# Modulation products of layer 0 issued for four weight pieces at a time

## The chip, the cores and the metric

The kernel runs on one core of one Trainium2 chip. The metric is the device time of one execution in microseconds (us); less is better. Three runs of the kernel before gave 1642.43 us in the median, 1640.19 at the lowest and 1645.79 at the highest.

## The reference, cut to what matters

Two layers work on 256 latent tokens (x) and 256 context tokens (ctx), each of 1024 channels. Every layer begins with the modulation: six vectors of 1024 for the latents and six for the context, which are products of one activated row each with the weight w_ada (1024 x 6144 for a layer).

```python
c_act = jax.nn.silu(c)
cc_act = jax.nn.silu(c_ctx)
for l in range(DEPTH):
    m_l = jnp.split((c_act @ w_ada[l] + b_ada[l])[:, None, :], 6, axis=-1)
    m_c = jnp.split((cc_act @ w_ada[l] + b_ada[l])[None, None, :], 6, axis=-1)
    h_l = modulate(rms_norm(x, norm_g[l, 0]), m_l[0], m_l[1])
    h_c = modulate(rms_norm(ctx, norm_g[l, 0]), m_c[0], m_c[1])
    y_l, y_c = token_mixer(h_l, h_c, w_in[l], ...)
    x = x + m_l[2] * rms_norm(y_l, norm_g[l, 1])
    h_l = modulate(rms_norm(x, norm_g[l, 2]), m_l[3], m_l[4])
    x = x + m_l[5] * rms_norm(sq_relu_mlp(h_l, w_mlp_up[l], w_mlp_down[l]), norm_g[l, 3])
```

The first two of the six vectors are needed before the token mixer, the other four only behind it. The token mixer runs three branches over one input projection: a gated linear recurrence (HGRN, 4 heads), differential attention (4 heads, two softmaxes each) and sliding-window attention; their gated outputs are merged and projected.

## The kernel before, in words

**Dense products.** A weight block of 2048 columns is loaded as two halves by SP's queue (L218). ACT copies the high part (`L227`), DVE takes the rest (`L228`), and TensorE runs three products for each tile of 128 channels (L249 to L251 with channels as output rows, L261 to L263 with tokens). These dense products fill PE nearly all the time. They write two banks of the accumulator in turn (`b_84`, `b_85` in the order listings); a bank can be written again when ACT has copied its content out.

**Mixers.** Beside the dense products of the next block run the chains of a mixer, issued by generators that take turns. The HGRN head walks seven levels: ACT copies (L776), PE multiplies (L783 on five levels, 32x32 groups; L786 on two, 128x128), DVE rescales in place what PE just read (L800), then the next level may start; L828 and L841 follow. The two heads of a pair run abreast. A differential head takes for each token tile two pairs of score products (L937, L938), a maximum (DVE L977), an exponential (ACT L898), the scaling and difference on DVE (L980, L981, L983), transposes (PE L989) and their copy (ACT L991). These small products use the other banks, `b_86` to `b_90`.

**Modulation.** Columns of w_ada come in three groups of 2048. Group 0 of layer 0 is done at the start. Groups 1 and 2 are spread over the weight blocks of layer 0's mixers: `weights` ends with `pump` (L349), which runs one entry of a list. An entry is one piece of w_ada, 128 rows by 1024 columns: `ada_load` (L385) takes two units of 512 columns from the arena A (33 units) and issues the load on SP's queue, and `ada_step` (L360) issues four products of 32x256 (L365), one for each column group j, into four row groups of the bank `b_91`. Every product is two instructions in the trace, so a piece is eight. After 16 pieces, `ada_done` (L428) copies the bank out. There are 34 entries (16 pieces and a done, twice) and 34 blocks.

**Order.** The arena gives out the units that were freed longest ago, in the order of the program; a unit that was freed by an instruction late in the program makes its next writer wait for it. The order in which each engine issues is made when the program is built: a scheduler takes the program's instructions as their inputs and buffers come ready. High priority (`hp`) moves evacuations and weight splits ahead.

Of the kernel before, what the change touches and what calls it, by code (L numbers as in the profile page):

```python
# [17 lines left out]
PSUM = bass.MemoryType.PSUM  # L18

D = 1024  # L20
T = 512
LAT = 256
DEPTH = 2
EPS = 1e-6
UNIT = 512
RAWS = 5
AHEAD = 100

O_DQ, O_DK, O_DV = 0, 512, 1024
# [83 lines left out]
class Net:  # L113
    def __init__(self, ctx, tc, ins, out):
        self.tc, self.nc = tc, tc.nc
        self.I, self.out = ins, out
        nc = self.nc
# [35 lines left out]
        self.exps = []  # L153
        self.pumps = []
        self.rate = 1
        self.ps = [pp.tile([128, 512], F32, tag=f"b{i}", name=f"b{i}") for i in range(8)]
# [23 lines left out]

# [1 line left out]
    def raw_slot(self):  # L182
# [4 lines left out]
    def set_fence(self, ops, skip, count):  # L187
        """the splits of weight blocks skip .. skip + count - 1 from here on are traced behind ops"""
        self.fence = [skip, count, ops]
# [7 lines left out]
    def weights(self, pieces, rope=0, dst=None):  # L197
        """a block of 2048 columns, loaded in halves; pieces(half): (view fn of the half, source AP); the first `rope`
        columns, in groups of 64 (axis, half, 16), are taken as (half, axis, 16)"""
        nc, tc = self.nc, self.tc  # L200
        if dst is None:
            self.wi += 1
            c = (self.wi % 2) * 4096
# [38 lines left out]
    def mm_cm(self, ps, w, nk, cc, act, t0, n, kt0=0, start=True, stop=True):  # L242
        """ps[128 channels, n tokens] = w[:, cc:cc+128]^T act"""
        nc = self.nc
        hi, lo = w
        for k in range(nk):
            xh, xl = act[kt0 + k]
            wh, wl = hi[:, k, cc:cc + 128], lo[:, k, cc:cc + 128]
            nc.tensor.matmul(ps, wh, xh[:, t0:t0 + n], start=start and k == 0, stop=False)  # L249
            nc.tensor.matmul(ps, wh, xl[:, t0:t0 + n], start=False, stop=False)  # L250
            nc.tensor.matmul(ps, wl, xh[:, t0:t0 + n], start=False, stop=stop and k == nk - 1)  # L251

    def mm_tm(self, ps, w, nk, c0, n, act, tt, kt0=0, start=True, stop=True):
        """ps[128 tokens, n] = act[:, tt]^T w[:, c0:c0+n]"""
        nc = self.nc
        hi, lo = w
        for k in range(nk):
            xh, xl = act[kt0 + k]
            xh, xl = xh[:, tt * 128:tt * 128 + 128], xl[:, tt * 128:tt * 128 + 128]
            wh, wl = hi[:, k, c0:c0 + n], lo[:, k, c0:c0 + n]  # L260
            nc.tensor.matmul(ps, xh, wh, start=start and k == 0, stop=False)  # L261
            nc.tensor.matmul(ps, xh, wl, start=False, stop=False)  # L262
            nc.tensor.matmul(ps, xl, wh, start=False, stop=stop and k == nk - 1)  # L263

# [1 line left out]
    def setup(self):  # L266
# [92 lines left out]

    def ada_step(self, l, g, half, k):  # L360
        nc = self.nc
        ca = self.CA.rearrange("p (k m) -> p k m", m=32)
        raw = self.ada_load(l, g, half, k)
        for j in range(4):
            nc.tensor.matmul(self.ps[7][32 * j:32 * j + 32, half * 256:half * 256 + 256], ca[:, k, :],  # L365
                             raw[:, j * 256:(j + 1) * 256], start=k == 0, stop=k == 7)
        raw.free()

    def ada_late(self, l, groups, ahead=2):
        """the groups of layer l on the vector engine; each step loads for a later one"""  # L370
        todo = [(g, half, k) for g in groups for half in range(2) for k in range(8)]
# [21 lines left out]
    def ada_acc(self, raw, k, acc):  # L393
        """sums over k of w * silu(c), by partition, one for each stream"""
        ca = self.CA.rearrange("p (k m) -> p k m", m=32)
# [49 lines left out]
    def mvec(self, l, s, i):  # L445
        """stream s: 0 latents, 1 context"""
        return self.M[l][:, s * 48 + i * 8:s * 48 + i * 8 + 8]

# [1 line left out]
    def rstd(self, ms, cols, add=True):  # L450
        """ms: mean squares, to which EPS is added unless it is in them"""
        r = self.sm(cols)
# [5 lines left out]
    def scale_vecs(self, l, sub, q=None):  # L458
        """of all channel tiles, or of q and 4 + q"""
        nc = self.nc  # L460
# [10 lines left out]
    def first_norm(self):  # L471
        """normalized and transposed x, channel tile k -> [128, 512]"""
        nc = self.nc
# [39 lines left out]
    def first_blocks(self, offs, evacs):  # L513
        """the first blocks of w_in[0]; channel tiles q and 4 + q are multiplied as soon as their modulation is known"""
        nc, tc = self.nc, self.tc
# [44 lines left out]
    def prenorm(self, tt, yb):  # L560
        """x[tt] / rms, transposed: the PSUM tiles of channels 0..511 and 512..1023"""
        nc = self.nc
# [23 lines left out]
    def modulate(self, tt, sv, tiles, yb, ops=(), quick=False):  # L586
        """the tiles of prenorm() to the activation of tokens tt; traced behind ops"""
        nc = self.nc
# [35 lines left out]
    def post(self, tt, y, yss):  # L624
        """x += y / rms, where y already holds the gains; yss [128, 5]: the shares of y's quarters in the mean
        square, and EPS"""
        nc = self.nc
# [9 lines left out]
    def tm_out(self, w, r0, act, y, yss, seqs, add, gains=None, after=None):  # L637
        """y[tt] (+)= act^T w[r0:r0 + 1024]; seqs: lists of (tokens, column blocks) worked through in turn; with gains,
        the mean squares of y are taken and y becomes y * gains(tt)"""
        nc = self.nc  # L640
# [25 lines left out]

# [1 line left out]
    def hgrn_dense(self, l, w, hp):  # L668
        """heads 2 hp and 2 hp + 1"""
        nc, A = self.nc, self.A  # L670
# [58 lines left out]
    def tm_pair(self, w, off, dst=None):  # L729
        """buffers, token tiles [128, 256] in them, and the function that fills those of a range"""  # L730
        bufs, v = self.pair_bufs(range(4))
# [13 lines left out]
    def hgrn_head(self, l, hd, s, v, gn, ys):  # L745
        """generator: one step of the chain at a time"""
        nc, A = self.nc, self.A
# [115 lines left out]
    def readout(self, ps, tiles, gain, ys):  # L863
        """per-tile rms norm of ps[128 tokens, tile, 128], gain, transpose, split"""
        nc, A = self.nc, self.A
# [29 lines left out]

# [1 line left out]
    def exp(self, out, in_, **kw):  # L897
        self.exps = self.exps[-3:] + [self.nc.scalar.activation(out, in_, AF.Exp, **kw)]  # L898

    def rope(self, t):  # L900
        """in place on the latent half of t [128, 512]; 64-row heads hold (half, axis, 16)"""
        nc, A = self.nc, self.A
# [9 lines left out]
    def stack_q(self, t, c, t0):  # L912
        """rows 64 c of t -> [128, tokens] with the high part there and the low part in the other rows"""
        nc = self.nc
# [6 lines left out]
    def stack_k(self, t):  # L921
        """high parts of both row halves, each doubled; low parts"""
        nc = self.nc
# [83 lines left out]

# [1 line left out]
    def swa_dense(self, l, w):  # L1009
# [49 lines left out]
    def swa_unit(self, l, tt, gp, S, K1, KL, v, ys):  # L1059
        """heads 2 gp, 2 gp + 1 of both groups for one token tile; column order (kv, g)"""  # L1060
        nc, A = self.nc, self.A
# [59 lines left out]

# [1 line left out]
    def gates(self, l, j, bufs=()):  # L1123
        """left as they are where the exponentials of a mixer run beside them; branch() takes the sigmoid then"""
        nc, A = self.nc, self.A
# [17 lines left out]
    def branch(self, l, j, ys, gates, merged, last):  # L1143
        """merged += gates * (ys^T w_branch[j])"""
        nc, I = self.nc, self.I
# [36 lines left out]
    def cm_blocks(self, loads, q0, skew, evac, done=lambda b: None, also=None):  # L1182
        """two channel tiles per block; skew: the first two blocks take the context half first, also()
        follows them in each half"""
        segs = [(q0, T - q0)]
# [31 lines left out]
    def pipeline(self, gens, depth):  # L1217
        """starts one generator per round, at most `depth` at a time"""
        gens, live = list(gens), []
# [9 lines left out]
    def layer(self, l):  # L1229
# [4 lines left out]
        tts = list(range(4)) if not last else [2, 3]  # L1234
        # token mixer
        ysb_b, ys_b = self.acts(4)
# [67 lines left out]
        for g in G.values():  # L1304
            g.free()
        # channel mixer
        q0 = 0 if not last else LAT
# [96 lines left out]
```

## Time and profile before

| | |
|---|---|
| median of three runs | 1642.43 us |
| lowest and highest | 1640.19 and 1645.79 us |
| span of the profiled execution | 1638.2 us |
| PE busy | 1596.6 us (97%) |
| DVE busy | 1082.4 us (66%) |
| ACT busy | 784.5 us (48%) |
| POOL busy | 387.9 us (24%) |
| chain that ended last, share of PE | 85% |
| mean DMA rate | 134 GB/s |

The profiled execution is given by its span alone, 1638.2 us; the median of the runs lies 4.2 us above that, and what lies around the span is not shown apart. Busy times are sums over the whole span; a share near 97% says that PE sets the time in most stretches, and the windows and waits say where it doesn't. In a timeline the first number is the start, the second the duration; matmuls overlap, so the cost of one in a row of them is the distance from its start to the next one's. A bracket at the end of a row tells how long the engine idled before it and who released it.

### The profile page before, as it was taken

The numbers are of one execution on the slowest core, as the hardware profiler recorded it, in microseconds if no ns is written. First come the engines' busy times: TensorE is split into PE (matmuls) and PEld (weight loads), VectorE is DVE, ScalarE is ACT, GpSimd is POOL, SyncE is SP. The second block draws the span as 40 slices with busy tenths as digits, with TensorE's granted clock in tenths as the row PEclk, the third lists the DMA queues.
The fourth block names the chain that finished last, engine by engine and source line by source line (L and its number), as shares of the span: only waits on it lengthen the run. The fifth ranks groups of instructions, "written<-read, shape, count | busy, mean of one in ns | idle before, by whom it ended". The sixth has DMA issues, their size and how long they took to land.

```text
span 1638.2 us, 30088 instructions
## 1 busy us (share of the span) xinstructions
PE 1596.6 (97%) x11806; PEld 1395.9 (85%) x11806; DVE 1082.4 (66%) x1974; ACT 784.5 (48%) x1648; POOL 387.9 (24%) x419
## 2 busy tenths in 40 slices
PE   6999999999999999999999999999999999989998
PEld 4788888787777679989898989999898888989998
DVE  4655534676466568777878756877768787765555
ACT  4443433455444457533324235754446655666554
POOL 1142415050410000310202011364455350121001
PEclk9999999999999999999999999999999999999999
DMA  9723243323432335465565524432434253436552
GB/s 279 227 79 116 79 142 103 93 63 116 132 97 55 106 113 184 149 208 174 174 187 186 177 82 143 141 104 78 130 104 104 76 157 104 155 121 188 182 181 91
DMA packets 234270, 220.26 MB, mean 134 GB/s; under 512 B 24400, under 2 KB 226320, under 8 KB 234128
## 3 DMA queue, kind: packets, MB, share of 16 engines
q1 hardware_dynamic: 234128, 218.34, 43.6%
q8 instruction: 92, 1.51, 0.4%
q14 instruction: 50, 0.41, 0.1%
HBM read 217.26 MB, written 1.05 MB: 133 GB/s over the span
## 4 chain that ended last, share of the span: by engine, by line
PE 85%; DVE 5%; POOL 4%; DMA 2%; issue 2%; ACT 2%; SPq 0%; DVEq 0%; POOLq 0%; ACTq 0%
PE b L249 15%; PE b L251 15%; PE b L250 15%; PE b L261 9%; PE b L263 8%; PE b L262 8%; PE b L938 2%; DMA arf<-in_w_ada_dram 1%; PE b L937 1%; POOL arf L907 1%; POOL arf L797 1%; PE b L1110 1%; PE b L365 1%; PE b L1097 1%; DVE whl L228 1%
## 5 line engine op out<-in xcount | busy, mean ns | idle before, releaser
L228 DVE TENSOR_TENSOR whl<-raw,whl 128x512 fp32r<-128x512 f32 x588 | 432.9, 757 | 217.3 <-ACT whl L227 205.1
L227 ACT CAST whl<-raw 128x512 fp32r<-128x512 f32 x588 | 356.3, 619 | 253.3 <-PE b L263 111.9
L249 PE MATMUL b<-h,whl 128*128 128x512 f32 (+1 forms) x1296 | 448.2, 347 | 0.4 <-ACT arf L741 0.2
L251 PE MATMUL b<-h,whl 128*128 128x512 f32 (+1 forms) x1296 | 446.1, 345 | 0.8 <-DVE whl L228 0.6
L250 PE MATMUL b<-h,whl 128*128 128x512 f32 (+1 forms) x1296 | 444.1, 343 | 0.0
L249 PEld LDWEIGHTS b<-h,whl 128*128 128x128 f32 x1296 | 247.0, 191 | 33.1 <-issue 2.7
L251 PEld LDWEIGHTS b<-h,whl 128*128 128x128 f32 x1296 | 246.3, 190 | 31.7 <-issue 3.4
L250 PEld LDWEIGHTS b<-h,whl 128*128 128x128 f32 x1296 | 246.4, 190 | 28.6 <-issue 3.3
L261 PE MATMUL b<-whl,arr 128*128 128x256 f32 x768 | 217.2, 284 | 0.0
L262 PE MATMUL b<-whl,arr 128*128 128x256 f32 x768 | 217.1, 283 | 0.0
L263 PE MATMUL b<-whl,arr 128*128 128x256 f32 x768 | 215.6, 283 | 1.0 <-DVE arr L1321 1.0
L1320 POOL TENSOR_TENSOR arf<-arf 128x256 f32<-128x256 f32 (+1 forms) x68 | 63.9, 939 | 425.1 <-ACT arr L1319 421.5
L261 PEld LDWEIGHTS b<-whl,arr 128*128 128x128 f32 x768 | 147.3, 192 | 1.3 <-DVE arf L653 0.8
L263 PEld LDWEIGHTS b<-whl,arr 128*128 128x128 f32 x768 | 146.6, 192 | 1.4 <-DVE arr L1321 1.4
L262 PEld LDWEIGHTS b<-whl,arr 128*128 128x128 f32 x768 | 147.4, 192 | 0.1
L261 PE MATMUL b<-whl,h 128*128 128x256 f32 x512 | 145.6, 286 | 0.0
L262 PE MATMUL b<-whl,h 128*128 128x256 f32 x512 | 145.4, 285 | 0.0
L263 PE MATMUL b<-whl,h 128*128 128x256 f32 x512 | 144.2, 285 | 0.0
L907 POOL TENSOR_TENSOR arf<-arf,cst 32x256 f32<-32x256 f32 x104 | 93.7, 901 | 204.9 <-DVE arf L983 80.9
L455 POOL TENSOR_TENSOR sm<-sm,nhalf 128x1 f32<-128x1 f32 (+2 forms) x42 | 32.3, 773 | 348.6 <-DVE sm L630 257.6
L404 DVE SCALAR_TENSOR_TENSOR arf<-arf,CA 128x1024 f32<-128x1024 f32 x84 | 110.0, 1355 | 5.3 <-DMA arf<-in_w_ada_dram 5.3
L261 PEld LDWEIGHTS b<-whl,h 128*128 128x128 f32 x512 | 97.8, 192 | 3.6 <-issue 1.2
(224 smaller groups left out, 2493.8 us busy)
## 6 DMA issues: line engine op xcount, KB each, us to landing
raw<-in_w_in_dram SPq DMA_DIRECT2D x110, 512.0 KB, 3.7
arf<-in_w_ada_dram SPq DMA_DIRECT2D x80, 512.0 KB, 4.7
raw<-in_w_mlp_down_dram SPq DMA_DIRECT2D x72, 512.0 KB, 3.9
raw<-in_w_mlp_up_dram SPq DMA_DIRECT2D x64, 512.0 KB, 3.8
raw<-in_w_out_dram SPq DMA_DIRECT2D x24, 512.0 KB, 3.4
arf<-in_w_ada_dram SPq DMA_DIRECT2D x32, 256.0 KB, 5.8
raw<-in_w_branch_dram SPq DMA_DIRECT2D x16, 512.0 KB, 3.7
raw<-in_w_in_dram SPq DMA_DIRECT2D x32, 128.0 KB, 2.9
```

Of the source, the lines that this page charges most:

```text
L227: self.behind(ops, lambda: nc.scalar.copy(r32(h), src))
L228: self.split_op = self.behind(ops, lambda: nc.vector.tensor_tensor(out=r32(l), in0=src, in1=h, op=ALU.subtract))
L249: nc.tensor.matmul(ps, wh, xh[:, t0:t0 + n], start=start and k == 0, stop=False)
L250: nc.tensor.matmul(ps, wh, xl[:, t0:t0 + n], start=False, stop=False)
L251: nc.tensor.matmul(ps, wl, xh[:, t0:t0 + n], start=False, stop=stop and k == nk - 1)
L261: nc.tensor.matmul(ps, xh, wh, start=start and k == 0, stop=False)
L262: nc.tensor.matmul(ps, xh, wl, start=False, stop=False)
L263: nc.tensor.matmul(ps, xl, wh, start=False, stop=stop and k == nk - 1)
L404: self.nc.vector.scalar_tensor_tensor(out=a[:, :], in0=raw[:, :], scalar=ca[:, k, s:s + 1], in1=a[:, :], op0=ALU.mult, op1=ALU.add)
L907: nc.gpsimd.tensor_tensor(out=b[o, 0:LAT], in0=x[i], in1=self.cst[i, C_RS:C_RS + LAT], op=ALU.mult)
L938: nc.tensor.matmul(ps[:, 0:nk], r32(S[own, q]), r32(KL[own, 0:nk]), start=False, stop=stop)
L1320: nc.gpsimd.tensor_tensor(out=r[:, c], in0=r[:, c], in1=r[:, c], op=ALU.mult)
```

## The change

A new constant `ADA_BATCH = 4` and a list of held pieces. An entry of the pump list loads its piece and returns, until four pieces are held; the fourth entry then issues the 16 products of all four, and frees each piece's units behind its products. A fourth of the blocks carries products, the other three only a load. The number of products, their operands, the bank and the loads are the same. Eight units of the arena are held at the most, where two were.

```diff
+ADA_BATCH = 4
...
+        self.ada_raws = []
...
     def ada_step(self, l, g, half, k):
         nc = self.nc
         ca = self.CA.rearrange("p (k m) -> p k m", m=32)
-        raw = self.ada_load(l, g, half, k)
-        for j in range(4):
-            nc.tensor.matmul(self.ps[7][32 * j:32 * j + 32, half * 256:half * 256 + 256], ca[:, k, :],
-                             raw[:, j * 256:(j + 1) * 256], start=k == 0, stop=k == 7)
-        raw.free()
+        self.ada_raws.append((k, self.ada_load(l, g, half, k)))
+        if len(self.ada_raws) < ADA_BATCH:
+            return
+        for k, raw in self.ada_raws:
+            for j in range(4):
+                nc.tensor.matmul(self.ps[7][32 * j:32 * j + 32, half * 256:half * 256 + 256], ca[:, k, :],
+                                 raw[:, j * 256:(j + 1) * 256], start=k == 0, stop=k == 7)
+            raw.free()
+        self.ada_raws = []
```

The lines of the changed kernel are numbered a little higher than those of the kernel before: L249 to L251 become L251 to L253, L365 becomes L371, L677 becomes L684, L783 and L786 become L790 and L793, L810 becomes L817, L828 becomes L835, L831 becomes L838, L841 becomes L848, L844 becomes L851, L937 and L938 become L944 and L945, L989 becomes L996.

Because other units are handed out, the order of other work changes too. PE in the HGRN levels of the first head pair, from the fifth level on (in these listings a name before the arrow is the bank that is written, `x4` counts products in a row). Before:

```order
L783 MATMUL b_87<-arf 32x32 x16
L783 MATMUL b_88<-arf 32x32 x16
L249 MATMUL b_84<-h,whl 128x512
L250 MATMUL b_84<-h,whl 128x512
L251 MATMUL b_84<-h,whl 128x512
L786 MATMUL b_89<-arf 128x128 x4
L249 MATMUL b_85<-h,whl 128x512
L250 MATMUL b_85<-h,whl 128x512
L251 MATMUL b_85<-h,whl 128x512
```

Here the levels stand apart, with dense products between them. With the change, from the fourth level on:

```order
L253 MATMUL b_84<-h,whl 128x512
L371 MATMUL b_91<-arf,CA 32x256 x8
L790 MATMUL b_90<-arf 32x32 x16
L790 MATMUL b_86<-arf 32x32 x16
L790 MATMUL b_87<-arf 32x32 x16
L790 MATMUL b_88<-arf 32x32 x16
L793 MATMUL b_89<-arf 128x128 x4
L793 MATMUL b_90<-arf 128x128 x4
L793 MATMUL b_86<-arf 128x128 x4
L793 MATMUL b_87<-arf 128x128 x4
L835 MATMUL b_88<-arf 128x128 x4
L835 MATMUL b_89<-arf 128x128 x4
```

The levels of both heads, to the L828 (now L835) behind them, stand behind one another with no dense product between them, where 77 stood between the same rows before; two w_ada pieces (L371) stand ahead of them.

ACT at the same place (L677, later L684, takes the sigmoid of a dense bank for the second head pair's gates and sets the bank free; L810, L831 and L844 copy the level products of the first pair). Before:

```order
L776 COPY arf<-arf 128x512 x8
L227 CAST whl<-raw 128x512 x4
L677 ACTIVATE arf<-b_84 128x512
L677 ACTIVATE arf<-b_85 128x512
L810 COPY arf<-b_89 128x512
L227 CAST whl<-raw 128x512 x2
L677 ACTIVATE arf<-b_84 128x512
L810 COPY arf<-b_90 128x512
L227 CAST whl<-raw 128x512 x2
```

With the change:

```order
L229 CAST whl<-raw 128x512
L817 COPY arf<-b_89 128x512
L817 COPY arf<-b_90 128x512
L838 COPY arf<-b_88 128x512
L838 COPY arf<-b_89 128x512
L684 ACTIVATE arf<-b_85 128x512
L851 COPY arf<-b_90 128x512
L684 ACTIVATE arf<-b_84 128x512
L851 COPY arf<-b_86 128x512
```

The gate sigmoids, which stood ahead of the first L810, now stand behind both L831 (L838 here): their output buffers are units that the first pair sets free late.

PE in the scores of the second pair of differential heads. Before:

```order
L937 MATMUL b_86<-arr 128x512
L938 MATMUL b_86<-arr 128x512
L251 MATMUL b_85<-h,whl 128x512
L937 MATMUL b_88<-arr 128x256
L938 MATMUL b_88<-arr 128x256
L249 MATMUL b_85<-h,whl 128x512
L250 MATMUL b_85<-h,whl 128x512
L251 MATMUL b_85<-h,whl 128x512
L937 MATMUL b_87<-arr 128x512
L938 MATMUL b_87<-arr 128x512
L249 MATMUL b_85<-h,whl 128x512
```

With the change:

```order
L371 MATMUL b_91<-arf,CA 32x256 x3
L944 MATMUL b_87<-arr 128x256
L945 MATMUL b_87<-arr 128x256
L944 MATMUL b_86<-arr 128x256
L945 MATMUL b_86<-arr 128x256
L944 MATMUL b_90<-arr 128x256
L945 MATMUL b_90<-arr 128x256
L944 MATMUL b_87<-arr 128x256
L945 MATMUL b_87<-arr 128x256
L944 MATMUL b_86<-arr 128x512
L945 MATMUL b_86<-arr 128x512
L996 MATMUL b_88<-cst,arf 128x128 x2
```

Dense products stood between the score pairs; now 14 pairs (8 of 256 and 6 of 512 columns), transposes of two at four places and eight products of w_ada stand between one dense product and the next.

Over the whole of PE, the rows of L365 are 33 before and 25 (L371) with the change. Runs of narrow products (32 or 64 output partitions, or L938 with its 64 rows) between products of 128 by 128 are 180 before and 164 with the change.

## Rows read from the trace of the kernel before

**Rows 1.** Windows: length; busy us of PE, PEld, DVE, ACT, POOL; clock; DMA.

```profile
372.00:404.00 32.00, 32.00 (x137) 21.80 (x138) 20.94 (x44) 17.85 (x47) 0.00 (x0) 1.00 0.36 111
...
1160.00:1163.30 3.30, 1.19 (x24) 0.91 (x22) 3.30 (x5) 1.47 (x4) 3.30 (x3) 1.00 0.52 157
1163.30:1170.20 6.90, 4.99 (x64) 4.45 (x65) 5.84 (x14) 1.79 (x4) 3.18 (x3) 0.51 0.23 77
```

**Rows 2.** Waits of PE, 100 to 640 us: total us, times, longest.

```profile
PE b L783 <- DVE arf L800: 2.8, 4, 1.2
```

**Rows 3.** Timeline of PE: start us, us, what ran; one piece alone.

```profile
249.42 0.39 PE L251 MATMUL b<-h,whl 128*128 128x512 f32 x1
249.74 0.64 PE L365 MATMUL b<-arf,CA 128*32 128x256 f32 x8
250.31 0.50 PE L249 MATMUL b<-h,whl 128*128 128x512 f32 x1
250.64 0.39 PE L250 MATMUL b<-h,whl 128*128 128x512 f32 x1
250.87 0.39 PE L251 MATMUL b<-h,whl 128*128 128x512 f32 x1
```

**Rows 4.** Timeline of PE: two pieces in one run.

```profile
433.82 1.07 PE L365 MATMUL b<-arf,CA 128*32 128x256 f32 x16
434.82 0.50 PE L249 MATMUL b<-h,whl 128*128 128x512 f32 x1
```

**Rows 5.** Timeline of PE: scores, and a piece behind them.

```profile
391.75 0.44 PE L989 MATMUL b<-cst,arf 128*128 128x128 f32 x2
391.94 0.47 PE L937 MATMUL b<-arr 128*128 128x512 f32 x1
392.34 0.49 PE L938 MATMUL b<-arr 64*128 64x512 f32 x1
392.76 0.64 PE L365 MATMUL b<-arf,CA 128*32 128x256 f32 x8
393.33 0.66 PE L989 MATMUL b<-cst,arf 128*128 128x128 f32 x4
```

**Rows 6.** Timeline of PE: one narrow score pair between dense products.

```profile
377.78 0.28 PE L937 MATMUL b<-arr 128*128 128x256 f32 x1
...
378.30 0.50 PE L250 MATMUL b<-h,whl 128*128 128x512 f32 x1
```

**Rows 7.** Timeline, HGRN levels of the first head pair.

```profile
112.11 0.68 DVE L800 TENSOR_TENSOR arf<-arf 128x512 f32<-128x512 f32 x1
...
112.91 0.68 DVE L800 TENSOR_TENSOR arf<-arf 128x512 f32<-128x512 f32 x1
112.94 0.46 PE L783 MATMUL b<-arf 128*32 128x32 f32 x32 [1.06 <-DVE arf L800]
...
113.64 0.46 PE L783 MATMUL b<-arf 128*32 128x32 f32 x32 [0.25 <-DVE arf L800]
```

**Rows 8.** Groups, 300 to 440 us: busy us, mean ns, idle before.

```profile
L977 DVE TENSOR_REDUCE sm<-b 128x1 f32<-128x512 f32 x16 | 11.0, 690 | 9.1 <-PE b L938 9.0
L898 ACT ACTIVATE arf<-b,sm 128x512 f32<-128x512 f32 x16 | 11.0, 694 | 7.3 <-DVE sm L977 7.3
L977 DVE TENSOR_REDUCE sm<-b 128x1 f32<-128x256 f32 x13 | 5.3, 423 | 4.6 <-PE b L938 4.4
L983 DVE SCALAR_TENSOR_TENSOR arf<-arf,sm 128x256 f32<-128x256 f32 x7 | 3.4, 481 | 0.1
L981 DVE TENSOR_SCALAR arf<-arf,sm,lam 128x256 f32<-128x256 f32 x7 | 2.9, 411 | 0.2
L980 DVE RECIPROCAL sm<-sm 128x2 f32<-128x2 f32 x15 | 2.4, 161 | 5.2 <-ACT arf L898 5.2
```

**Rows 9.** Page, part 5: a weight split on DVE.

```profile
L228 DVE TENSOR_TENSOR whl<-raw,whl 128x512 fp32r<-128x512 f32 x588 | 432.9, 757 | 217.3 <-ACT whl L227 205.1
```

**Rows 10.** Source L365: who waited, us and times.

```profile
  DMA arf<-in_w_ada_dram: 0.7, 2
```

## The prediction

> **What bounds the kernel now.** I read the windows first, then the waits, then timelines. In a differential stretch of layer 0, PE is busy 32.00 of 32.00 us, DVE 20.94 and ACT 17.85, at clock 1.00 [rows 1]. So in the part that the change touches, PE's issue of products is the time, and a matmul costs its distance to the next one. A wait appears only where a chain runs out of cover: from 100 to 640 us PE waited 2.8 us, four times, for the HGRN rescaling on DVE [rows 2]. What such a place costs once nothing covers it is seen in layer 1: PE busy 1.19 of 3.30 us and, in the 6.90 us behind that, a granted clock of 0.51, nearly the lower of the two levels, 1.2 GHz [rows 1]. The median of the runs, 1642.4, lies 4.2 above the profiled span of 1638.2; I work against the span and add the sum to the median.
>
> **Term 1, switches between shapes: a gain.** A lone piece takes 0.32 us to enter (249.42 to 249.74), 0.57 inside and 0.33 to leave, where the two dense distances it replaces are 0.23 each: 0.89 + 0.33 - 0.46 = 0.76 us [rows 3]. Two pieces in one run take 1.00 inside [rows 4], so the second piece adds 0.43 and each run costs 0.76 - 0.43 = 0.33 for its two switches. The number of products does not change; only runs are saved. If the change did all it says, 32 pieces would make 8 runs, 24 fewer, 7.9 us. The order listing gives 25 rows of w_ada products instead of 33, and counted with all other narrow products, 164 runs instead of 180: 16 fewer. A piece behind a narrow score product costs only its inner 0.57 (392.76 to 393.33) [rows 5], 0.19 less than alone, so merging there saves less. I take 12 runs at 0.33 and 4 at 0.19: **-4.7** (ends: 16 x 0.33 = -5.3, 16 x 0.19 = -3.0).
>
> **Term 2, the first HGRN pair: a loss.** Six more arena units are held, so the next pair's gates get units that the first pair frees late. ACT's sigmoids, which empty the dense banks, therefore queue behind both L831, and the dense products that wait for these banks can't fill the levels. The bare levels: DVE needs 0.80 from one head's rescaling to the next (112.11 to 112.91), 1.60 for two heads, PE 2 x 0.46 [rows 7]; idle 0.68 for each level step. I count two such steps and as much as one more for the steps with longer products, 2.0. Of the idle there now, 1.06 + 0.25 [rows 7], 1.3 falls into the same place and is not paid twice: **+0.7**. Least: the two w_ada pieces ahead, 1.00 us [rows 4], cover the first step and the 1.3 vanish: -1.3. Most: the bare place of layer 1, idle 3.30 - 1.19 = 2.1, and half of the next 4.99 busy us lost to the clock, 2.5 [rows 1]: +4.6.
>
> **Term 3, the second HGRN pair.** It is bunched over some levels, but its order stays mixed with dense products; **0**, with the rest of the present waits, 2.8 - 1.3 = 1.5 [rows 2], as the end on either side.
>
> **Term 4, scores of the second differential pair: a loss.** There 14 score pairs stand without dense products, and the dense product behind them needs a bank that ACT empties behind the eleventh exponential. DVE's work until that exponential's maximum, counted in the change's order: eight maxima of 256 columns at 0.42, three of 512 at 0.69, four scalings at 0.41, three differences at 0.48, four reciprocals at 0.16 [rows 8] and one weight split at 0.76 [rows 9], 9.9 us. Then the exponential, 0.69 [rows 8], and the copy of the bank, of the same shape, taken as 0.69: 11.3 from the first score on. PE has in that time six pairs of 512 at 0.82 (391.94 to 392.76) [rows 5], seven of 256 at 0.52 (377.78 to 378.30) less two halves done earlier, 3.2 [rows 6], seven products of w_ada, 1.0, and four double transposes at 0.19 [rows 5]: 9.9. The difference is 1.4; **+1.5**. Least 0: DVE starts some maxima before the last dense products are through. Most: PE's products at the dense distance of 0.23 [rows 3], 6 x 0.46 + 7 x 0.23 + 1.8 = 6.2, so +5.1.
>
> The Trainium skill, Perfetto Trace Analysis, section Optimization Strategy, says that interleaving regimes with different contended engines may help; this change takes DVE-bound scores and PE-bound dense products apart. By that rule nothing of DVE's excess would be hidden in PE's switches, the term would be its upper end, and the sum about +1.6.
>
> **Term 5, sliding window.** Three score units stand together there, with w_ada products between them, so DVE lags by less: **+0.5**, from 0 to half of the differential end, 2.6.
>
> **Term 6, loads.** SP issues the same 32 loads, five in a row, and the weight loads pass them by; the first three of a batch have up to three blocks to land. The fourth is used at once, as each is now; PE waited for such a load 0.7 us in all, twice [rows 10]. Nothing is taken: **0** (from -0.7 to +1.4, twice that). What covers it is the dense run ahead; without it the wait is at PE's head and all dense products queue behind.
>
> **Sum:** -4.7 + 0.7 + 0 + 1.5 + 0.5 + 0 = **-2.0**, so 1636.2 for the span and **1640.4 us** for the median. The ends together: -8.8 and +12.2.
>
> **Rivals.**
> *A, slower: the bared stretches cost the clock.* Place: the first HGRN pair and the second differential pair. Terms 2 and 4 then take their upper ends, and the second place loses 2.5 to the clock as in layer 1: 3.9 + 3.6 + 2.5 = 10.0 more, **1650.4**. It decides if a bared place becomes as empty as that one in layer 1, with PE busy 1.19 of 3.30 [rows 1]. For it: the order shows no dense product in 14 score pairs. Against: my sum has PE busy 9.9 of 11.3. Chance 0.15.
>
> *B, faster: the chains stay hidden.* DVE keeps ahead, the 2.8 us of waits go, and all 16 runs save 0.33: -5.3 - 2.8 - 0.7, **1633.6**. For it: DVE is busy two thirds of a dense stretch [rows 1]. Chance 0.13.
>
> *C: it hardly batches.* The scheduler takes the products as loads and buffers come, so runs stay apart, the gain is the least, -3.0, and the losses hold: **1642.1**. For it: 25 rows where 8 were meant. Chance 0.12.
>
> *D, slower: a gap at each batch.* Every time eight units are held, some evacuation waits for a late unit, and PE stops as it does now, 1.3 us [rows 7], eight times: 10.5 - 4.7 = +5.8, **1648.2**. Against: the order shows dense products moved away at three places, not eight. Chance 0.10. The Trainium skill, Perfetto Trace Analysis, section Optimization Strategy, says that consistent bubbles "can mean there isn't enough SBUF/PSUM for the next tile to be allocated"; by it this would be the likeliest rival.
>
> **How the numbers follow.** The forecast has 0.50. A measurement here can tell about 0.3%, 4.9 us, from no change, so the bounds are 1637.5 and 1647.3. Faster is B and a small part of the forecast's lower tail, 0.13 + 0.04 = **0.17**. Slower is A and D and 0.03 of the forecast's upper tail, **0.28**. Same is the rest, **0.55**. The range reaches from 1636.0, short of B, to 1650.0, beyond D and just short of A.
>
> **What would show it.** In the changed profile: the w_ada products in runs of 8 to 16 with one entry of about 0.32 us (term 1); a wait of PE L790 on DVE L807 in one block, 2 us or so, with no dense product between (term 2); idle of one to two microseconds at L944 in the second differential pair (term 4); no wait of L371 on DMA (term 6). I am wrong if the clock falls to half in layer 0's mixers (A), if PE idles at every batch, on ACT's evacuations (D), or if no bare stretch shows more idle than now (B).

## The result, and the profile after

The change made the kernel slower: 1666.11 us in the median of 4 runs (1665.38 to 1666.74) against 1641.31 for the kernel before on the same chip, a ratio of 1.015 (95% interval 1.0134 to 1.0166). The forecast was 1640.4 with a range to 1650.0; the time lies 16 us beyond the range. The profiled execution has a span of 1665.0 us, 26.8 more than before.

The waits of PE in the changed kernel from 60 to 660 us, layer 0's mixers (total us, times, longest):

```profile
PE b L790 <- DVE arf L807: 12.3, 5, 5.0
PE b L944 <- ACT arf L905: 2.3, 3, 0.9
```

The first line answers to [rows 2]: 2.8 us have become 12.3, and one wait alone lasts 5.0. The windows of two stretches with a fallen clock, and of the 11 us around the first (length; busy us of PE, PEld, DVE, ACT, POOL; clock; DMA):

```profile
117.50:124.30 6.80, 5.12 (x140) 4.68 (x141) 5.58 (x14) 0.42 (x1) 0.00 (x0) 0.50 0.40 115
397.40:414.40 17.00, 15.61 (x32) 7.97 (x32) 10.74 (x27) 7.91 (x25) 0.00 (x0) 0.50 0.19 63
112.00:123.00 11.00, 4.86 (x151) 3.76 (x150) 10.58 (x16) 3.27 (x7) 5.31 (x4) 0.75 0.37 98
```

In 11 us of the first HGRN pair PE is busy 4.86, and DVE 10.58. Behind the 5.0 us gap the clock is at 0.50, as it was in layer 1 [rows 1], and it is so again for 17.0 us in the scores of the second differential pair, though PE is busy 15.61 of them. In [rows 1] a differential stretch had 32.00 of 32.00 at clock 1.00.

Where the 26.8 us are, counted over PE: the time in which no matmul ran, and, for each row of the clock at 0.5, half of PE's busy time in it (an estimate, and on the high side: what a wait-bound chain would take at full clock anyway is in it too).

| | before | after |
|---|---|---|
| idle, 60 to 300 us | 3.1 | 14.2 |
| idle, 300 to 660 us | 0.3 | 6.2 |
| idle elsewhere | 38.3 | 38.4 |
| half clock, 60 to 300 us | 0 | 5.6 |
| half clock, 300 to 660 us | 0 | 10.9 |
| half clock elsewhere | 11.3 | 9.4 |
| the rest of the span | 1585.3 | 1580.4 |

Idle gained 17.1, the clock 14.6, and the rest lost 4.9: 26.8. The rest, in which the saved switches would be, fell by about what term 1 had forecast, but it is no measure of the switches, as the account of term 1 says; idle and clock took more than six times as much.

**What stands at the start of the first stall.** POOL's level products (L797, now L804) of the first HGRN pair. Before, with the second w_ada piece and ACT's level copies ahead of them:

```profile
84.54 0.64 PE L365 MATMUL b<-arf,CA 128*32 128x256 f32 x8
...
85.44 1.46 ACT L776 COPY arf<-arf 128x512 f32<-128x512 f32 x2
...
86.44 2.80 POOL L797 TENSOR_TENSOR arf<-arf 128x512 f32<-128x512 f32 x2 [11.62 <-ACT arf L776]
...
101.39 9.05 POOL L797 TENSOR_TENSOR arf<-arf 128x512 f32<-128x512 f32 x7
...
109.62 2.56 DVE L228 TENSOR_TENSOR whl<-raw,whl 128x512 fp32r<-128x512 f32 x3 [1.91 <-ACT whl L227]
```

After, POOL and what ACT and DVE do just ahead of it (L724 forms a readout gate, L783 copies a level's operand):

```profile
95.06 0.42 DVE L724 TENSOR_TENSOR arf<-b,arf 128x256 f32<-128x256 f32 x1 [0.79 <-ACT arf L723]
...
96.20 0.85 ACT L783 COPY arf<-arf 128x512 f32<-128x512 f32 x1
...
97.19 1.55 POOL L804 TENSOR_TENSOR arf<-arf 128x512 f32<-128x512 f32 x1 [0.88 <-ACT arf L783]
...
102.36 14.94 POOL L804 TENSOR_TENSOR arf<-arf 128x512 f32<-128x512 f32 x11
```

The second copy of the level operands starts only behind the readout gates, and POOL 10.8 us later (97.19 against 86.44). From the arena's order in the program: before, it wrote a unit of the second w_ada piece, whose products ran at 84.54, just ahead of it; now that piece is held, and the longest free units are the temporaries of the readout gates. POOL then still has eleven products of some 1.4 us to do at 102 us, where it had seven. What follows, on DVE and PE:

```profile
112.09 4.32 DVE L230 TENSOR_TENSOR whl<-raw,whl 128x512 fp32r<-128x512 f32 x3 [4.06 <-ACT whl L229]
...
116.33 1.53 DVE L807 TENSOR_TENSOR arf<-arf 128x512 f32<-128x512 f32 x1
...
117.98 0.68 DVE L807 TENSOR_TENSOR arf<-arf 128x512 f32<-128x512 f32 x1
...
118.00 1.36 PE L790 MATMUL b<-arf 128*32 128x32 f32 x64 [4.96 <-DVE arf L807]
...
118.78 0.68 DVE L230 TENSOR_TENSOR whl<-raw,whl 128x512 fp32r<-128x512 f32 x1
```

ACT does the weight copies L229 in turn with level copies that wait for POOL, so DVE waits 4.06 us for them; its three splits then take 4.32 us beside POOL, where three took 2.56 before, most of it behind POOL's end at 110.44; the rescaling L807 takes 1.53, where [rows 7] have 0.68. PE, out of dense products by then, waits 4.96 us for it. No instruction that the change adds is slow here: it is the cover that is gone and POOL's work that now falls on DVE's. The Trainium skill, SBUF — State Buffer, section SBUF: two separate sides, says that a DVE instruction with two SBUF inputs and a GpSimd instruction that reads SBUF hold a pair of ports one at a time: "the other fully blocks". The durations here, 1.44 us for a split beside POOL and 0.68 without, agree.

Why PE is out of dense products stands in ACT's rows. The next dense products need the banks that the sigmoid of the second pair's gates empties (L677, now L684). Before:

```profile
113.52 0.60 ACT L677 ACTIVATE arf<-b 128x512 f32<-128x512 f32 x1 [1.21 <-PE b L783]
```

After, it comes behind both L838, 16 us later, as term 2 had read from the order:

```profile
129.17 0.58 ACT L838 COPY arf<-b 128x512 f32<-128x512 f32 x1 [0.51 <-PE b L835]
129.65 0.60 ACT L684 ACTIVATE arf<-b 128x512 f32<-128x512 f32 x1
```

The second HGRN pair has the same form: a wait of 3.11 us behind a rescaling, and 3.07 behind three splits of 3.39 us beside POOL.

```profile
198.77 1.63 DVE L807 TENSOR_TENSOR arf<-arf 128x512 f32<-128x512 f32 x1
...
200.55 0.47 PE L790 MATMUL b<-arf 128*32 128x32 f32 x32 [3.11 <-DVE arf L807]
...
205.88 3.39 DVE L230 TENSOR_TENSOR whl<-raw,whl 128x512 fp32r<-128x512 f32 x3
...
210.02 2.26 PE L790 MATMUL b<-arf 128*32 128x32 f32 x96 [3.07 <-DVE arf L807]
```

In the second differential pair PE waits little at a time, then the clock falls in the middle of the chain and products take up to twice as long (a pair of 512 columns, 398.54 to 399.99, takes 1.45 us where [rows 5] have 0.82):

```profile
395.52 0.39 PE L944 MATMUL b<-arr 128*128 128x256 f32 x1 [0.71 <-ACT arf L905]
...
396.85 0.38 PE L944 MATMUL b<-arr 128*128 128x256 f32 x1 [0.63 <-ACT arf L905]
...
398.54 0.79 PE L944 MATMUL b<-arr 128*128 128x512 f32 x1
399.26 0.79 PE L945 MATMUL b<-arr 64*128 64x512 f32 x1
399.99 0.69 PE L996 MATMUL b<-cst,arf 128*128 128x128 f32 x2
```

The first two w_ada pieces run together as the change says, as 16 instructions behind one entry of 0.32 us, and all waits for loads together are 0.4 us, where [rows 10] have 0.7. Over the whole trace the batches came apart: the 32 pieces make 25 runs, as the order said, and twelve of these have only two to six instructions.

```profile
111.65 0.39 PE L253 MATMUL b<-h,whl 128*128 128x512 f32 x1
111.97 1.07 PE L371 MATMUL b<-arf,CA 128*32 128x256 f32 x16
...
391.82 0.62 PE L371 MATMUL b<-arf,CA 128*32 128x256 f32 x2
392.37 0.38 PE L945 MATMUL b<-arr 64*128 64x256 f32 x1
```

From the view of that line, its waits (us, times):

```profile
  DMA arf<-in_w_ada_dram: 0.4, 1
```

### The profile page after: what moved, and what is told of

Its sections match the earlier page's. It is cut to its first block, busy times and chain, and to the rows that moved or that the text cites. A ratio compares the mean times of both kernels' runs of the same rounds, so it can differ in the third digit from the quotient of the medians.

```text
span 1665.0 us, 30113 instructions
## 1 busy us (share of the span) xinstructions
PE 1606.2 (96%) x11806; PEld 1404.8 (84%) x11806; DVE 1091.5 (66%) x1974; ACT 784.2 (47%) x1648; POOL 392.6 (24%) x419
## 4 chain that ended last, share of the span: by engine, by line
PE 73%; DVE 4%; POOL 3%; ACT 1%; issue 1%; DVEq 0%; POOLq 0%; ACTq 0%
PE b L251 12%; PE b L253 12%; PE b L252 12%; PE b L263 8%; PE b L264 8%; PE b L265 8%; POOL arf L914 2%; PE b L945 2%; PE b L944 1%; PE b L1117 1%; PE b L1104 1%; PE b L1009 1%; DVE whl L230 1%; PE b L996 1%; POOL arf L915 0%
## 5 line engine op out<-in xcount | busy, mean ns | idle before, releaser
L229 ACT CAST whl<-raw 128x512 fp32r<-128x512 f32 x588 | 356.9, 619 | 265.4 <-PE b L265 113.0
L251 PE MATMUL b<-h,whl 128*128 128x512 f32 (+1 forms) x1296 | 449.4, 348 | 0.3 <-ACT arf L748 0.2
L253 PE MATMUL b<-h,whl 128*128 128x512 f32 (+1 forms) x1296 | 447.2, 345 | 0.8 <-DVE whl L230 0.6
L251 PEld LDWEIGHTS b<-h,whl 128*128 128x128 f32 x1296 | 248.5, 192 | 32.2 <-issue 2.6
L253 PEld LDWEIGHTS b<-h,whl 128*128 128x128 f32 x1296 | 247.4, 191 | 30.5 <-issue 2.9
```

What stands on the lines that cost most here:

```text
L229: self.behind(ops, lambda: nc.scalar.copy(r32(h), src))
```

## The experiments

The first theory, M, was that the held units make the stalls; G, that the grouping does. With e9 came two on how the held units do it in the first HGRN pair: P, that the level copies get late units and POOL starts late; S, that the gates of the second pair do and their sigmoids come late. Times are medians; those of before are 1640.6 to 1641.2 us in these comparisons. "Rest" is the last line of the table above.

**e1, hold only.** The products as before, the units set free by fours.

```diff
-        raw.free()
+        self.ada_raws.append(raw)
+        if len(self.ada_raws) == ADA_BATCH:
+            for raw in self.ada_raws:
+                raw.free()
+            self.ada_raws = []
```

> Each piece's four products are issued at once, as before, but its two units are set free only when four pieces are held. Theory M (the held units make the evacuations of dense banks late; bared chains, idle PE, fallen clock): as slow as the change or somewhat more, 1664 to 1672 us, since the switches saved (about 4.7 us) are missing. Theory G (it is the grouped products themselves that push other work apart): like before, 1639 to 1644 us.

Measured 1666.1 us, 1.0155 (1.014 to 1.017): the whole loss, without one grouped product. The same stall stands at the same place (waits of PE):

```profile
PE b L790 <- DVE arf L807: 14.2, 8, 5.7
```

So the held units make the loss, and the grouping is not needed for it. It was as slow as the change, not 4.7 us slower, so the grouping is worth less than term 1 gave it: the rest is 1581.9, against 1580.4 with grouping and 1585.3 before.

**e2, second group only.**

```diff
+        if len(self.ada_raws) < (ADA_BATCH if g == 2 else 1):
```

> Pieces are held and multiplied by fours only for the second group (the second half of the pieces); the first group as before. Theory M: what the profile of the change shows before 300 us goes (idle 12.5 against 3 us now, and two stretches of half clock, 5.5 us), what it shows behind 390 us stays: 1649 to 1656 us. Theory G: half of the loss, as half of the products are grouped: about 1653 us; the two are told apart here by the places, not by the sum.

Measured 1647.6 us, 1.0046 (1.0029 to 1.0062), a loss of 7.1 us. Idle before 300 us is back at 3.1 with no fallen clock; from 300 to 660 us it has 4.0 idle and 4.6 by the clock. It is 1.4 us below the first theory's range, and its places are those of that theory, though the low clock in the second differential pair lasts 3.4 us there and not 17.0.

**e3, two at a time.** `ADA_BATCH = 2`.

> Two pieces at a time instead of four: four units held at the most. Theory M: the loss goes with the units held beyond what the arena can spare, and the order of PE shows only short bared stretches here: 1640 to 1647 us. Theory G: a loss of half the change's, about 1653 us.

Measured 1648.6 us, 1.0047 (1.0032 to 1.0062): a third of the loss, between the two theories and nearer the first. One stall of 2.9 us in the second HGRN pair remains. In the second differential pair the clock falls although PE has hardly idled ahead of it, and PE doesn't idle at all while it is low:

```profile
380.00:386.70 6.70, 6.48 (x27) 4.25 (x25) 6.27 (x16) 3.89 (x13) 0.00 (x0) 1.00 0.53 158
386.70:396.90 10.20, 10.20 (x22) 6.16 (x22) 7.05 (x18) 4.73 (x15) 0.00 (x0) 0.50 0.18 52
```

**e4, the change with buffers taken earlier.**

```diff
+        if l == 0 and hp == 0:
+            self.kx1 = [A.get(2) for _ in range(2)]
...
+            if l == 0:
+                self.early = [A.get(1) for _ in range(4 if hp == 0 else 2)]
```

> The change as it is (four pieces held and grouped), but the units of three sets of buffers are taken earlier in the program, when units that have long been free are still to be had: the gates of the second HGRN pair, queries and keys of the second differential pair, keys and values of the window attention. Theory M: the idle and the fallen clock of the first HGRN pair and of the second differential pair go (8.5 and 10.5 us by the change's profile, with some of the second HGRN pair's 9.5), those of the window attention stay: 1640 to 1650 us. Theory G: nothing is won, 1662 to 1668 us.

Measured 1656.7 us, 1.0097 (1.0082 to 1.0113): 9.4 us better than the change, 7 above the range. Idle before 300 us was still 9.8, against 14.2. My reading at that point, that the late sigmoids of the next pair's gates were the whole cause, doesn't hold: those units were given early here, and a stall in the first pair stayed. But it is not refuted either. The sigmoids are early again (lines are numbered three higher in this kernel, so they are L687), and the longest wait of that pair falls from 4.96 to 2.07 us although POOL starts even later than in the change:

```profile
99.72 1.52 POOL L807 TENSOR_TENSOR arf<-arf 128x512 f32<-128x512 f32 x1 [3.08 <-ACT arf L786]
...
108.72 0.59 ACT L687 ACTIVATE arf<-b 128x512 f32<-128x512 f32 x1
...
116.29 0.46 PE L793 MATMUL b<-arf 128*32 128x32 f32 x32 [2.07 <-DVE arf L810]
```

The window of that stretch before, in the change and in e4:

```profile
60.00:130.00 70.00, 68.63 (x773) 59.14 (x772) 44.23 (x75) 33.58 (x60) 27.91 (x28) 1.00 0.35 109
60.00:130.00 70.00, 63.72 (x753) 56.20 (x752) 50.79 (x82) 31.23 (x57) 31.00 (x28) 0.95 0.35 105
60.00:130.00 70.00, 66.82 (x714) 57.01 (x714) 50.27 (x71) 32.44 (x59) 26.34 (x20) 0.98 0.36 111
```

PE idles 1.4, 6.3 and 3.2 us of it. So of the 4.9 us that the change adds, 3.1 went when the sigmoids were early, and 1.8 stayed with POOL late. The division is not a clean one, because e4 takes other buffers early too.

**e5, nothing held across heads.** What is held is multiplied and freed before heads start.

```diff
     def run(self, *gens):
+        self.ada_flush()
```

> As the change, but the pieces that are held are multiplied and set free before the generators of a mixer's heads start, so no piece is held while heads take their buffers in the program; groups are of one to four pieces. Theory M (units held across the heads' buffers): the other buffers get units about as long free as before, idle and clock fall back to about those of before, and some of the switches are saved (174 runs against 180, 2 us): 1637 to 1643 us. If grouping in itself did harm: above 1648 us.

Measured 1654.8 us, 1.0083 (1.0069 to 1.0096): wrong by 12 us. The first pair still had a stall of 4.3 us. That sent me to POOL's start: 97.71 us here too. By the program's order the two pieces are freed before the heads, but behind the readout gates' temporaries, and the arena gives the longest free first, so the level copies still got the temporaries; e9 and e10 try that.

**e6 and e7, the same four units set apart, products single and by twos.**

```diff
+            self.blk = self.A.get(4)
+            self.P = Arena(self.arf, self.blk.i * UNIT, 4)
```

> Four units of the arena are set apart for the pieces all through layer 0's mixers; products of each piece at once, as before. Pair with the next: same units, other grouping. Theory M: some bared stretches are in the order of PE (24, 23 and 20 rows), so 1643 to 1652 us.

> The same four units set apart, products of two pieces together. Theory M: the same bared stretches as in the run before this one, less the saved switches (170 runs against 175, 1 to 2 us): within 3 us of it, on the lower side. Theory G (grouping pushes other work apart): 5 us or more above it.

Measured 1654.9 us (1.0084, 1.0069 to 1.0098) and 1654.1 (1.0077, 1.0059 to 1.0095). e6 is 3 us above its range; with the units alike, grouping made no difference that these runs can tell.

**e8, the kernel before with buffers taken earlier**, as in e4, and four of the last gates.

> The kernel before, pieces one by one, with units taken earlier in the program for four sets of buffers of layer 0: gates of the second HGRN pair, queries and keys of the second differential pair, keys and values of the window attention, four of the last gates. Theory M: at most the 3.4 us that PE idles in layer 0's mixers can be won: 1637 to 1641 us; if units held for longer do harm as in the change, 1643 us or more.

Measured 1644.5 us, 1.0022 (1.0013 to 1.0031): above the range of a gain. Taking units early holds them longer, and that costs too.

**e9, the change with the first two pieces done at once.**

```diff
+        if len(self.ada_raws) < (1 if (g, half) == (1, 0) and k < 2 else ADA_BATCH) and k < 7:
```

> The change, but the first two pieces are multiplied and set free at once; the others by fours (the last of a half by two). Theory P (in the first HGRN pair the first level copies take units freed late, by the readout gates, where they took the units of these two pieces before; so POOL's level products start at 97 us instead of 86 and everything behind runs late): POOL starts its level products near 86 us, the idle and fallen clock from 110 to 125 us (6.0 and 2.5 us) go, the rest of the change's loss stays: 1654 to 1660 us. Theory S (the gates' sigmoids of the second pair, late by their own units, empty the dense banks late): nothing of it goes, 1664 to 1668 us.

Measured 1654.2 us, 1.0079 (1.0065 to 1.0093): 11.9 us better than the change. POOL starts 1.5 us later than before and not 10.8, PE is busy 68.45 of the 70 us from 60 to 130, and the clock there is 1.00. But the first sigmoid comes early again too, so P and S go together here. The timeline of POOL and ACT:

```profile
87.92 2.80 POOL L804 TENSOR_TENSOR arf<-arf 128x512 f32<-128x512 f32 x2 [10.24 <-ACT arf L783]
...
115.00 0.60 ACT L684 ACTIVATE arf<-b 128x512 f32<-128x512 f32 x1 [1.16 <-PE b L790]
```

and the window:

```profile
60.00:130.00 70.00, 68.45 (x770) 58.75 (x769) 44.95 (x79) 34.20 (x61) 27.89 (x28) 1.00 0.39 120
```

**e10, the kernel before, with the first two pieces' units freed two pieces later.**

```diff
+        if (g, half) != (1, 0) or k not in (0, 1):
+            for raw in self.ada_raws:
+                raw.free()
+            self.ada_raws = []
```

> The kernel before, but the units of the first two pieces are set free two pieces later, behind the first HGRN pair's buffers in the program; all products at once. Theory P: the loss of that place alone, with POOL's level products starting near 97 us: 1641 + 8 = 1647 to 1651 us, nearly all of it before 130 us. Theory S: like before, within 2 us, as the gates of the second pair have the units they had, or others free as long.

Measured 1646.2 us, 1.0034 (1.0021 to 1.0047): a loss of 5.1 us from four units and no other edit, 1 us under the range. POOL's start, the splits beside it and the wait are about those of the change. The sigmoid is as late as there:

```profile
97.46 1.53 POOL L804 TENSOR_TENSOR arf<-arf 128x512 f32<-128x512 f32 x1 [0.90 <-ACT arf L783]
...
112.15 4.31 DVE L230 TENSOR_TENSOR whl<-raw,whl 128x512 fp32r<-128x512 f32 x3 [4.06 <-ACT whl L229]
...
116.38 1.53 DVE L807 TENSOR_TENSOR arf<-arf 128x512 f32<-128x512 f32 x1
...
118.06 1.36 PE L790 MATMUL b<-arf 128*32 128x32 f32 x64 [5.69 <-DVE arf L807]
...
130.59 0.60 ACT L684 ACTIVATE arf<-b 128x512 f32<-128x512 f32 x1
```

The window of that stretch:

```profile
60.00:130.00 70.00, 63.10 (x745) 55.42 (x743) 47.78 (x75) 29.52 (x54) 29.97 (x28) 0.93 0.34 104
```

What was expected for S rested on gates that keep their units. They don't: followed through the program, the arena gives them units 27, 28, 23 and 24 here and in the change, and 25, 26, 20 and 21 in the kernel before and in e9. So neither e9 nor e10 tells P from S; that four units held a little longer make this stall, they do show. By the count of the table this place costs 5.5 us idle and 3.7 by the clock more than before, and the run lost only 5.1: the count for the clock is too high here.

**e11, the same for the fifth to seventh piece**, `k not in (4, 5, 6)`.

> The kernel before, but the units of the fifth, sixth and seventh piece are set free behind the second HGRN pair's buffers; all products at once. Theory P for the second pair: its place alone, idle and clock of the change there are 6.5 and 3.0 us against 1.5 us idle before, so 1641 + 8 = 1646 to 1651 us, nearly all of it between 180 and 230 us. If only the first pair's place matters: like before.

Measured 1654.1 us, 1.0080 (1.0067 to 1.0093): a loss of 13.0, more than expected. The second HGRN pair has its part (PE busy 53.26 of 60 us), and the differential pair, which I hadn't counted in, a clock at 0.5 for 13.6 us and 2.6 us idle. Two windows, the first as before, the second that of the second pair:

```profile
60.00:130.00 70.00, 68.45 (x769) 58.72 (x768) 45.23 (x78) 34.67 (x62) 28.45 (x28) 1.00 0.37 114
...
180.00:240.00 60.00, 53.26 (x633) 43.59 (x632) 40.13 (x65) 22.16 (x39) 24.09 (x24) 0.89 0.33 100
```

The three places of holding, e10, e11 and e2, lose 5.1, 13.0 and 7.1 us, 25.2 together; e1, which holds everywhere, loses 25.6. That they add up so well is in part luck: e2 groups too, and both e11 and e2 have a part in the second differential pair.

**e12, grouping where no heads take buffers meanwhile.**

```diff
+        if len(self.ada_raws) == (ADA_BATCH if (g, half) == (1, 1) else 1) or k == 7:
```

> Grouping only where no heads take buffers while a piece is held: the eight pieces of the second half of the first group by fours, and what is held is multiplied before heads start; all others one by one. Theory M and P: no added idle, a few switches saved (176 runs against 180, about 1 us): 1637 to 1642 us. If grouping itself harms: 1645 us or more.

Measured 1639.2 us against 1641.2, 0.9992 (0.9981 to 1.0002): no difference that can be told. The profiled execution, one of the longer ones at 1642.7 us, has idle of 4.6 us from 60 to 300 us against 3.1, and 3.4 us at clock 0.50, so "no added idle" did not quite come true. PE's waits for L811, the rescaling there, are as [rows 2], 2.8 us, four times:

```profile
PE b L794 <- DVE arf L811: 2.8, 4, 1.2
```

No version ran clearly faster than the kernel before.

## Why the prediction was wrong

**The sign and the size.** I forecast no change with a gain of 2.0 us; it was a loss of 25. The rival that came nearest is A: bared stretches that cost the clock, 1650.4 us with a chance of 0.15. Its mechanism is what the profile shows, in four places and not two, and without its condition: in the second differential pair PE was busy 15.61 of 17.00 us and not 1.19 of 3.30. D, a gap at each batch, is not what happened: the stalls stand at the head pairs. The rule of the Trainium skill that was named there (Perfetto Trace Analysis, section Optimization Strategy: consistent bubbles can mean that there isn't enough SBUF) holds in so far as e1 makes the stalls by holding units alone; they are not at each batch.

**Term 1, switches, -4.7.** The rest of the span fell by 4.9, but e1 shows 3.4 of that with no product grouped; what grouping adds is 1.5 between e1 and the change, and 1.0 between e6 and e7, by a count with an estimate for the clock in it. So the agreement is luck, and the term was too large. Counted from the rows of the w_ada products alone (from the start of the product ahead to that of the second one behind, less 0.46 and the idle time, as in the term), 33 runs cost 24.5 us before and 25 runs 23.3 in the change: an estimate of 1.2 us saved. A run of two instructions takes 0.55 us inside (391.82 to 392.37), about as long as one of eight with 0.57, so a batch that comes apart saves little. Why the rest fell in e1, whose order has 179 runs of narrow products where the change has 164, is open; the estimate for the clock is large in both and may hold it.

**Term 2, first HGRN pair, +0.7.** This is the step that failed first, in its size. That the gates' sigmoids queue behind both L838 and bare the levels came true (129.65 against 113.52). But the term took the bare levels as a chain of PE and the rescaling alone, 0.80 us a head. It left out what else stands in DVE's and ACT's queues at that place: the three weight splits between two rescalings, the copies ahead of them, and POOL, whose late start slows both. The waits came to 6.0 us, and the clock to 2.5 by the count: idle rose by 4.9 us from 60 to 130 us. I had followed one late buffer, the next pair's gates, and missed another: the first pair's own level copies took late units as well. e4 says that both matter, e9 and e10 move them together, and what each costs alone is not shown. The end of the range that I gave, +4.6, was read from a place where the clock fell, but not with that queue ahead of it.

**Term 3, second HGRN pair, 0.** Taken as hidden because the order stayed mixed with dense products. It had 6.5 us of waits (3.1 and 3.1 the two longest) and 3.0 by the clock. An order that is mixed says nothing about a wait whose engine starts late.

**Term 4, second differential pair, +1.5.** Idle was 2.7, which is near and below the upper end of 5.1; the clock at 0.5 for 17.0 us, 7.8 us by the count, was left to rival A. The clock was taken to hold as long as PE was mostly busy; it fell all the same.

**Term 5, window attention, +0.5**: 3.4 idle (1.6 of it in the stretch whose clock fell, 570 to 585 us) and 3.0 by the clock. **Term 6, loads, 0**: right, 0.4 us against 0.7.

So the sum failed on terms 2 to 5, which had +2.7 us for bared stretches: by the count, which is on the high side for the clock, idle rose by 17 us and the clock took 16 from 60 to 660 us; the switches saved about 1.

Not settled: why the clock falls and stays low so long in the second differential pair. The kernels that hold units have it to different lengths there (17.0 us in the change, 13.6 in e11, 10.2 in e3, 3.4 in e2), and none was run that keeps PE filled with dense products in that place while all else stays.

## What to carry to other kernels

Where buffers come from an arena that gives out the longest free unit, holding a few units longer changes the place of every later buffer; ask of each chain that starts in that time which engine freed the unit that it now gets, and when. Count a chain with all that stands in its engines' queues (weight splits, copies, the third engine beside them), not with its own instructions alone. What saves tenths of a microsecond may bare stretches that cost the TensorE clock for several microseconds, so the clock belongs in the sum wherever the order shows PE without its filling work. And where two experiments move two suspects together, look in the trace for one that moves only one of them.

## What the runs showed that I had not expected

A weight split on DVE takes 0.68 us alone and about 1.44 us while POOL works (4.32 us for three, in the change), so POOL, busy 24% of the span and late by 10.8 us, has a part in PE's gap of 5.0 us; the other part is the late sigmoids that leave PE nothing else to do.

The clock fell to 0.50 in a stretch in which PE was busy 15.61 of 17.00 us with score products. The idle just ahead of it was two waits of 0.71 and 0.63 us, about as much as the 1.06 and 0.25 [rows 7] of the kernel before, behind which the clock stayed up. In e3 one wait of 0.2 us stood ahead, and the clock was at 0.50 for 10.2 us in which PE never idled. So PE's busy time in a profile did not tell here whether the clock would hold; in e3, three score pairs and a transpose stood in a row just ahead of the fall (383.62 to 386.67), with no dense product between them.
